# Splitting streamed weights into two parts: the low part by a negated copy and an adding transfer instead of a vector subtraction

## The chip, the cores and the metric

The kernel runs on one core of one Trainium2 chip. The metric is the device time of one execution in microseconds (us); lower is better. The kernel before took 1412.06 us (median of 3 runs, 1411.49 to 1412.78).

## The reference, cut to what matters

One inference step of a two-layer decoder trunk. 512 prompt tokens and 64 sample tokens (8 sequences of 8) go through it together as 576 columns. Each layer does

```
x = x + W_out . [SSD | sliding-window attention | HGRN2 | RG-LRU](W_in . RMSNorm(x))
x = x + W_down . square(relu(W_up . RMSNorm(x)))
```

with a model dimension of 1024, an input projection of 22 tiles of 128 columns (and four single columns), an output projection of 1024 x 1024 and a hidden layer of 4096. A final RMSNorm follows. All inputs are float32, and results are asked for in nearly full float32 precision. Caches and states of all four mixers are read and written too.

## The kernel before, in words

**The split.** A big product is done in the type float32r, which keeps fewer bits than float32. So that little is lost, each operand is written as hi + lo: hi is the operand rounded to float32r, lo is operand - hi. The product is then three matmuls, hi.hi, hi.lo and lo.hi, added up in PSUM. `product()` (L326 to L345) does this: for each half of the columns (288 of 576) it goes over the blocks of the contraction, and for each block it issues `wh.xh`, `wh.xl`, `wl.xh` in this order.

**The weights.** They stream from HBM in tiles of 128 x 1024 float32 (512 KB). `raw()` (L308) allocates a tile `raw` of a ring of WRAW = 3 buffers and loads it on the sync engine's queue. `weight()` (L315 to L324) allocates `hi` and `lo` of rings of WHL = 2 buffers and fills them with two instructions, both on line 323: ScalarE copies `raw` into `hi` (the store rounds), and VectorE subtracts `hi` from `raw` into `lo`. One such tile feeds 48 matmuls of 288 columns. "Plain" weights are those that go through `weight()`: 22 tiles of W_in, 8 of W_out, the first 6 of W_up and 32 of W_down per layer, without the last two of the second layer (these are split in `last_down()`): 134 in all. The other W_up tiles go through `up_pair()` (L1058), which forms a seven-product scheme with buffers of its own (`uh`, `ul`, `vh`, `vl`); it takes its raw tiles from the same ring.

**The order of the work.** A tile framework allocates the buffers, sets all semaphores, and orders each engine's instructions by a priority list; each engine then runs its own list in order. Both instructions of line 323 stand under `high_priority(HP)`, so they go ahead of other work that is ready at the time. Small loads and all stores but the last go through `dma()` (L167), on GpSimd's queue (POOL). A GpSimd instruction that waits holds up everything behind it on that engine.

**The stages.** Layer 0: mixers up to about 298 us (first projections and the norm, HGRN2 for one head pair, SSD, HGRN2 for the other pair, RG-LRU, attention, output projection), then its MLP up to about 709 us. Layer 1: mixers up to about 987 us, MLP and final norm to the end. In the mixers, the projections' products (`pi`) are mixed on TensorE with many small float32 matmuls of the mixers; in the MLP, groups of W_up products (`pu`, then `p`) alternate with groups of four W_down tiles (`pd`, 192 matmuls).

**The start.** The first weight (`w0`) is split before the norm: `norm()` (L356) is told to place its work behind the two instructions kept in `split_ins`; this is an order of issue, since in the trace the first norm activation starts before the first subtraction does. The first two products run ahead of 1/rms, which is worked out beside them.

Of the kernel before, what the change touches and what calls it, by code (L numbers as in the profile page):

```python
# [10 lines left out]
F32 = mybir.dt.float32  # L11
# [3 lines left out]
ALU = mybir.AluOpType  # L15
AX = mybir.AxisListType
PSUM = bass.MemoryType.PSUM
DRAM = bass.MemoryType.DRAM

DEPTH = 2  # L20
NP_ = 512                # prompt tokens
NB, NT = 8, 8            # sample sequences, tokens of each
NS = NB * NT
T = NP_ + NS             # token columns
# [5 lines left out]
NEG = -1e30  # L30
CW = 600                 # columns of a causal convolution over the padded row
PADW = CW + 3
SLOT = 608
WRAW, WHL = 3, 2
# [3 lines left out]
GROUPS = (288, 288)            # of columns at the end  # L38
AHEAD = 4
SQB = 2  # L40
ORDER = (0, 4, 1, 5, 2, 6, 3, 7)      # of the model dimension's tiles, as their products come
# [5 lines left out]
# columns of the packed per-layer vectors  # L47
# [9 lines left out]
# columns of the constants  # L57
# [7 lines left out]
# tiles of 128 columns of w_in, in the order of their use  # L65
# [48 lines left out]
class Pool:  # L114
    """A pool of tiles by role: t(tag) allocates the next tile of that role."""
# [15 lines left out]
def seqs(t, w=NT):  # L131
    """the sample columns as [rows, sequence, w]; w = 11 in padded rows"""
    o = NP_ if w == NT else NP_ + 3
    return t[:, o : o + NB * w].rearrange("p (b t) -> p b t", b=NB)


def staggered(parts):
    """run the parts' steps so that each part is one step behind the one before it"""
    n = 0
    while parts:  # L140
        n += 1
        for p in parts[:n]:
            if next(p, True):
                parts.remove(p)
                n -= 1


class Kern:
# [14 lines left out]
    # ---- small helpers  # L163
# [3 lines left out]
    def dma(self, dst, src):  # L167
        """a transfer that the first loads go before"""
        with self.tc.issue_after(self.gate):
            self.q(QS).dma_start(dst, src)  # L170
# [21 lines left out]
    # ---- constants and everything that is loaded once  # L192
# [36 lines left out]
    def spill(self):  # L229
        """the residual goes to DRAM while the mixers use its place"""  # L230
# [7 lines left out]
    def rel_bias(self):  # L238
        """bias[t, h, s] of a query t and the keys s of its own and the previous block, NEG outside the window."""
# [22 lines left out]
    def rel_bias_rows(self):  # L262
        nc, dma, (sel, newmask, skew) = self.nc, self.dma, self.rel
        for i in range(2):
# [3 lines left out]
            # sample rows (r, e, t) of 32-row groups: sequence b = 4 * u + r, head 2 * i + e  # L268
# [11 lines left out]
    def lower_bounds(self):  # L280
        """log of HGRN's lower bound of layer 1 and of its complement (layer 0's bound is zero by construction)."""
# [11 lines left out]
        V.tensor_tensor(t[1], t[1], t[3], op=ALU.mult)      # p0  # L293
        V.tensor_tensor(t[2], t[2], t[3], op=ALU.mult)      # p1
        V.tensor_tensor(t[3], t[1], t[2], op=ALU.add)
        V.tensor_tensor(t[3], t[3], t[1], op=ALU.subtract)
        V.tensor_scalar(t[3], t[3], 0.0, None, op0=ALU.max)  # lb
        V.tensor_scalar(t[4], t[3], -1.0, 1.0, op0=ALU.mult, op1=ALU.add)
        V.tensor_scalar(t[4], t[4], 0.0, None, op0=ALU.max)  # 1 - lb
# [7 lines left out]
    # ---- weights: float32 = hi + lo, both exact in float32r; eight blocks of 128 x 128  # L307
# [7 lines left out]
    def weight(self, src, raw=None):  # L315
# [6 lines left out]
        with self.tc.high_priority(HP):  # L322
            self.split_ins = nc.scalar.copy(hi, raw).ins, nc.vector.tensor_tensor(lo, raw, hi.bitcast(F32), op=ALU.subtract).ins  # L323
        return hi, lo  # L324

    def product(self, name, blocks, put):  # L326
        """put(half, columns, sum over the blocks (wh, wl, xh, xl) of w.T @ x in that half of the columns);
        behind a norm the first products run ahead of 1/rms, which their put() needs"""
# [21 lines left out]
    def exp_ln(self, ins):  # L350
        """the tables of exp and ln again, behind the last use of others"""
# [3 lines left out]
    # ---- RMSNorm over the model dimension: split (x * w) for the products, 1/rms as a factor of their results  # L355
# [31 lines left out]
    def rstd(self, r, sqs, scale, ones):  # L387
        """r = (mean over features + eps)^-1/2, on every partition; ones adds the rows that belong together."""
# [8 lines left out]
    # ---- input projection of one tile of columns -> [128, T] in PSUM, times 1/rms into dst  # L397
# [38 lines left out]
    def history(self, xp, hist, out):  # L436
        """the padded row's history columns, and the last three columns of each sequence as the new history"""
# [14 lines left out]
    def to_tokens(self, src, dst):  # L452
        """[128 features, T] -> tokens on partitions, [128, 4 x 128 | 128], the last block with 64 rows"""
# [10 lines left out]
    def by_sequence(self, dst, src):  # L464
        """dst [64, b, n] = src [64 tokens, n] in the rows of sequence b, else 0"""
# [4 lines left out]
    # ---- HGRN2, one pair of heads  # L470
    def hgrn_begin(self):
        P = self.hp = Pool(self, f"hgrn{self.li}", reuse_waits="tile")
        # zero-padded: entries outside a level's pattern stay zero
# [11 lines left out]
    def hgrn(self, p):  # L485
# [6 lines left out]
        # log sigmoid(f), log f, k  # L492
# [17 lines left out]
        # v with tokens on partitions  # L510
        vt = P.t("vt", 640)
        self.to_tokens(v, vt)
        # the diagonal: (q_t . k_t) v_t
# [8 lines left out]
        # pairs (s, t) by the level at which their blocks meet; every exponent is <= 0  # L522
# [37 lines left out]
        # c is now the running sum within a chunk  # L560
# [11 lines left out]
        # states  # L572
# [16 lines left out]
        # o  # L589
# [9 lines left out]
        # samples  # L599
# [16 lines left out]
        # the norm by head, the gate  # L616
# [8 lines left out]
    # ---- SSD  # L625
# [3 lines left out]
    def ssd_dt(self):  # L629
        """dt, the running sum of dt * A, and exp(last - sum): rows = heads"""  # L630
# [27 lines left out]
        # tokens on partitions: [128, chunk, (dt | sum | exp(last - sum)), head]  # L658
# [9 lines left out]
        # C's factor exp(sum) for the two heads of a group, and its last values  # L668
# [12 lines left out]
    def ssd(self):  # L681
# [29 lines left out]
        for g in range(2):  # L711
            rg = slice(64 * g, 64 * g + 64)
            # decay[s, t] = exp(sum_t - sum_s) where t >= s, times B_s . C_t
# [17 lines left out]
            # exp(min(., 0))  # L731
# [5 lines left out]
            # tokens on partitions: x dt, x dt exp(last - sum)  # L737
# [16 lines left out]
            # the states before each chunk and after the last one  # L754
# [19 lines left out]
            # y  # L774
# [32 lines left out]
    # ---- RG-LRU  # L807
    def lru(self, xps, gs):
# [4 lines left out]
        # -8 softplus(-lambda)  # L813
# [12 lines left out]
        for p, xp in enumerate(xps):  # L826
# [8 lines left out]
            V.tensor_scalar(r[:, p, :CW], r[:, p, :CW], lr[:, p : p + 1], None, op0=ALU.mult)      # log a  # L835
        # gelu's tanh
# [13 lines left out]
        # 1 - a^2 = tanh(-log a) (1 + a^2)  # L850
# [6 lines left out]
        # the column before a sample's first token carries its state  # L857
# [15 lines left out]
    # ---- sliding-window attention; q tile e holds heads (e, 2 + e) on the partitions of kv heads (0, 1)  # L873
    def swa(self, Q, K, Vv):
# [23 lines left out]
        # samples: rows (r, e, t) in groups of 32, blocks (i, u), sequence b = 4 * u + r  # L898
# [7 lines left out]
        Ls = [P.t("L", [2, 256], bufs=4) for _ in range(2)]      # by kv head  # L906
# [31 lines left out]
        p2 = self.bank("aos")                            # [128 (i d), u, r, 32]  # L938
# [9 lines left out]
        # prompt, by blocks of queries  # L948
# [3 lines left out]
        def block(nb):  # L952
# [3 lines left out]
            L = [P.t("L", [2, 256], bufs=4) for _ in range(2)]       # by kv head  # L956
# [44 lines left out]
    # ---- output projection of two mixers' tiles  # L1001
# [26 lines left out]
    # ---- MLP; its first product by the seven products of Winograd's form, quadrants of 2 feature halves x 2 column halves  # L1028
    def quads(self, P):
        """x * w in split quadrants: T1 = B12 - B11 in the place of B12, T2 = B22 - T1, T3 = B22 - B12, T4 = B21 - T2"""  # L1030
# [27 lines left out]
    def up_pair(self, P, i, Q, rstd):  # L1058
        """squared relu of two tiles of the hidden layer"""
# [9 lines left out]
        with self.tc.high_priority(HP):  # L1069
            a = split(hl("u", 8, 3), ra)                                       # A11 | A12  # L1070
            s = P.t("s", [8, 128])
            V.tensor_tensor(s[:, :4], rb[:, :4], rb[:, 4:], op=ALU.add)         # S1 = A21 + A22
# [308 lines left out]
```

## Time and profile before

| what | value |
|---|---|
| median of 3 runs | 1412.06 us |
| span of the profiled execution | 1412.2 us |
| TensorE (PE) matmuls | 1388.7 us, 98% |
| TensorE weight loads (PEld) | 1326.4 us, 94% |
| VectorE (DVE) | 1031.7 us, 73% |
| ScalarE (ACT) | 651.7 us, 46% |
| GpSimd (POOL) | 64.6 us, 5% |
| sync engine's DMA queue | 102.12 MB, 21.2% of the 16 DMA engines' span |
| GpSimd's DMA queue | 22.65 MB, 4.7% |

The profiled execution's span is 0.1 us above the median of the runs, so a sum made against the span stands for the median too. A busy share is an average over stages with different limits. Matmuls overlap in the pipeline: a busy time of 296 ns for one does not mean that the next one starts 296 ns later, so the count of matmuls in a stretch tells more than their busy time.

### The profile page before, as it was taken

The page shows a single profiled execution, that of the slowest core. Times are in us where ns is not written, and L with a number is a line of the kernel's source. Part 1 is how long each engine was busy: PE and PEld are TensorE (multiplying, and loading weights), DVE is VectorE, ACT ScalarE, POOL GpSimd, SP SyncE. Part 2 cuts the span into 40 slices and gives each one's busy share as a digit, 9 for nine tenths or more (in the row PEclk, how much of TensorE's full clock was granted, in tenths as well). Part 3 has the DMA queues.
Part 4 walks back from the last instruction along what each step waited for, and adds up shares of the span by engine and source line. Part 5 has one row for each costly group of instructions (what it writes and reads, how often), then busy time and mean ns, then how long its engine had stood idle before and what let it go on. Part 6 is the DMA issues. An engine that isn't in the chain of part 4 may idle for free.

```text
span 1412.2 us, 25457 instructions
## 1 busy us (share of the span) xinstructions
PE 1388.7 (98%) x10376; PEld 1326.4 (94%) x10376; DVE 1031.7 (73%) x2059; ACT 651.7 (46%) x1167; POOL 64.6 (5%) x125
## 2 busy tenths in 40 slices
PE   7999999999999999999999999999999999999997
PEld 7898889899999999999998989898999999999997
DVE  7966687668777778777668768764886877778765
ACT  6455427566433344333453734456662433343334
POOL 4010101100000000000000000010000000000000
PEclk9999999999999999999999999999999999999999
DMA  7142323312232223232330323130232223223221
GB/s 252 47 145 101 103 72 103 99 58 89 79 103 93 88 76 105 75 104 85 125 128 27 118 77 107 66 136 31 83 113 75 76 91 105 80 72 105 90 75 67
DMA packets 39716, 131.33 MB, mean 93 GB/s; under 512 B 5960, under 2 KB 8128, under 8 KB 39568
## 3 DMA queue, kind: packets, MB, share of 16 engines
q1 hardware_dynamic: 29312, 102.12, 21.2%
q0 software_dynamic: 6544, 22.65, 4.7%
q10 hardware_dynamic: 3744, 4.95, 1.0%
q8 instruction: 81, 1.33, 0.4%
q14 instruction: 35, 0.29, 0.1%
HBM read 120.32 MB, written 11.34 MB: 93 GB/s over the span
## 4 chain that ended last, share of the span: by engine, by line
PE 90%; DVE 4%; ACT 3%; issue 1%; DMA 1%; DVEq 0%; ACTq 0%
PE pd L336 33%; PE p L1089 21%; PE pi L336 16%; PE pu L336 5%; PE sc L544 2%; PE pl L1241 2%; PE ss L393 1%; PE ao L993 1%; PE y L781 1%; PE pdt L336 1%; PE o L595 1%; DMA cs<-acd 1%; PE os L605 1%; ACT hi L323 1%; PE ys L791 1%
## 5 line engine op out<-in xcount | busy, mean ns | idle before, releaser
L336 PE MATMUL pd<-fh,hi 128*128 128x288 f32 x960 | 283.8, 296 | 0.0
L336 PE MATMUL pd<-fl,hi 128*128 128x288 f32 x960 | 283.7, 296 | 0.0
L336 PE MATMUL pd<-fh,lo 128*128 128x288 f32 x960 | 283.6, 295 | 0.0
L323 ACT CAST hi<-raw 128x1024 fp32r<-128x1024 f32 x134 | 140.3, 1047 | 287.2 <-PE pd L336 154.6
L336 PE MATMUL pi<-xh,hi 128*128 128x288 f32 x704 | 213.4, 304 | 7.4 <-ACT xh L368 7.4
L336 PE MATMUL pi<-xl,hi 128*128 128x288 f32 x704 | 214.0, 304 | 0.7 <-DVE xl L369 0.7
L336 PE MATMUL pi<-xh,lo 128*128 128x288 f32 x704 | 213.9, 304 | 0.0
L323 DVE TENSOR_TENSOR lo<-raw,hi 128x1024 fp32r<-128x1024 f32 x134 | 163.6, 1221 | 24.3 <-ACT hi L323 23.4
L336 PEld LDWEIGHTS pd<-fh,hi 128*128 128x128 f32 x960 | 181.1, 189 | 0.0
L336 PEld LDWEIGHTS pd<-fl,hi 128*128 128x128 f32 x960 | 181.0, 189 | 0.0
L336 PEld LDWEIGHTS pd<-fh,lo 128*128 128x128 f32 x960 | 180.6, 188 | 0.0
L1024 DVE TENSOR_TENSOR x<-x,pd 128x288 f32<-128x288 f32 x240 | 107.9, 450 | 99.5 <-PE pd L336 99.3
L336 PEld LDWEIGHTS pi<-xh,hi 128*128 128x128 f32 x704 | 136.1, 194 | 11.7 <-ACT xh L368 7.4
L336 PEld LDWEIGHTS pi<-xh,lo 128*128 128x128 f32 x704 | 136.2, 193 | 4.2 <-issue 3.2
L336 PEld LDWEIGHTS pi<-xl,hi 128*128 128x128 f32 x704 | 135.9, 193 | 2.9 <-DVE xl L369 1.2
L1089 PE MATMUL p<-Th,ul 128*128 128x288 f32 x312 | 92.0, 295 | 0.0
L1089 PE MATMUL p<-Th,uh 128*128 128x288 f32 x312 | 92.0, 295 | 0.0
L1089 PE MATMUL p<-Tl,uh 128*128 128x288 f32 x312 | 92.0, 295 | 0.0
L1089 PE MATMUL p<-xh,ul 128*128 128x288 f32 x312 | 91.9, 295 | 0.0
L1089 PE MATMUL p<-xl,uh 128*128 128x288 f32 x312 | 91.7, 294 | 0.0
L1089 PE MATMUL p<-xh,uh 128*128 128x288 f32 x312 | 91.7, 294 | 0.0
L1065 ACT CAST uh<-raw 128x1024 fp32r<-128x1024 f32 x52 | 54.5, 1048 | 66.8 <-PE p L1089 44.1
(487 smaller groups left out, 3114.1 us busy)
## 6 DMA issues: line engine op xcount, KB each, us to landing
raw<-in_wu SPq DMA_DIRECT2D x64, 512.0 KB, 3.2
raw<-in_wd SPq DMA_DIRECT2D x64, 512.0 KB, 4.3
raw<-in_wi SPq DMA_DIRECT2D x44, 512.0 KB, 3.3
raw<-in_wo SPq DMA_DIRECT2D x16, 512.0 KB, 3.2
x<-in_xT SPq DMA_DIRECT2D x8, 288.0 KB, 5.5
a<-acd ACTq DMA_DIRECT2D x4, 576.0 KB, 3.9
xl<-in_xT POOLq DMA_DIRECT2D x8, 288.0 KB, 4.2
xd<-x POOLq DMA_DIRECT2D x8, 288.0 KB, 2.4
```

The costliest lines, as they stand in the source:

```text
L323: self.split_ins = nc.scalar.copy(hi, raw).ins, nc.vector.tensor_tensor(lo, raw, hi.bitcast(F32), op=ALU.subtract).ins
L336: self.nc.tensor.matmul(out, w, x[:, a], start=n == 0, stop=n == last)
L393: nc.tensor.matmul(ps[:, :TH], ones, s[:, TH * h : TH * h + TH], start=n == 0, stop=n == len(sqs) - 1)
L544: nc.tensor.matmul(pv[:, :, 64 * ci : 64 * ci + 64], kE[:, 128 * ci : 128 * ci + 128], qE[:, :, 64 * ci : 64 * ci + 64], start=True, stop= ...
L595: nc.tensor.matmul(ps[r, a], vt[:, 128 * ci + 64 * d : 128 * ci + 64 * d + 64], A[:, d, a], start=True, stop=ci == 0)
L605: nc.tensor.matmul(p2[r, NT * b : NT * b + NT], S0[r, b], q[r, NP_ + NT * b : NP_ + NT * b + NT], start=False, stop=b == NB - 1)
L781: nc.tensor.matmul(ps[r, a], xs[:, 128 * ci + 64 * j : 128 * ci + 64 * j + 64], D[j][:, a], start=True, stop=ci == 0)
L791: nc.tensor.matmul(p2[r, NT * b : NT * b + NT], S0T[rg, b, j], self.cs[j][rg, a], start=False, stop=b == NB - 1)
L1024: self.nc.vector.tensor_tensor(y[:, a], x[:, a], ps, op=ALU.add)
L1065: S.copy(hl[0], src)
L1089: nc.tensor.matmul(ps[:, :TH], u, x, start=j == 0, stop=j == 11)
L1241: nc.tensor.matmul(ps, u[:, o + q], v[:, a], start=j == 0, stop=j == 11)
```

## The change

The subtraction on VectorE goes. ScalarE writes `lo` as the rounded weights times -1, reading `raw` a second time. Then GpSimd issues a transfer from SBUF to SBUF that adds `raw` onto `lo`, so that `lo` = raw - hi. `split_ins` now holds ScalarE's copy and that transfer. The rings grow: 4 raw tiles and 3 pairs of hi and lo, which is 12 KB more of each SBUF partition; the space that the program reserves for GpSimd's DMA descriptors is set to 4096 bytes per partition. The rest of the diff removes comments.

```diff
-WRAW, WHL = 3, 2
+WRAW, WHL = 4, 3
...
         with self.tc.high_priority(HP):
-            self.split_ins = nc.scalar.copy(hi, raw).ins, nc.vector.tensor_tensor(lo, raw, hi.bitcast(F32), op=ALU.subtract).ins
+            first = nc.scalar.copy(hi, raw).ins
+
+            nc.scalar.mul(lo, raw, -1.0)
+            self.split_ins = first, nc.gpsimd.dma_start(lo, raw, accum_op=ALU.add).ins
         return hi, lo
...
-    nc = _bacc.Bacc("TRN2", target_bir_lowering=False, num_devices=1)
+    nc = _bacc.Bacc("TRN2", target_bir_lowering=False, num_devices=1, dynamic_dma_scratch_size=4096)
```

## Rows read from the trace of the kernel before

**Rows 1.** The page: span, and busy time of each engine.

```profile
span 1412.2 us, 25457 instructions
PE 1388.7 (98%) x10376; PEld 1326.4 (94%) x10376; DVE 1031.7 (73%) x2059; ACT 651.7 (46%) x1167; POOL 64.6 (5%) x125
```

**Rows 2.** Windows by stage: length, busy us (count) of five engines, clock, DMA share, GB/s.

```profile
0.00:298.00 298.00, 285.17 (x2100) 254.71 (x2100) 211.23 (x491) 154.13 (x301) 39.50 (x75) 0.97 0.33 113
298.00:709.00 411.00, 411.00 (x3092) 410.55 (x3092) 310.87 (x561) 172.98 (x285) 7.10 (x13) 1.00 0.27 92
709.00:987.00 278.00, 275.56 (x2065) 246.03 (x2064) 194.17 (x431) 143.72 (x275) 17.96 (x37) 0.97 0.25 84
987.00:1412.00 425.00, 416.96 (x3126) 415.15 (x3124) 315.47 (x578) 180.88 (x306) 0.00 (x0) 0.99 0.25 86
```

**Rows 3.** The chain that ended last, two pieces of layer 0's MLP: start, us, what.

```profile
371.80 25.49 PE pd L336 x192
397.29 22.30 PE p L1089 x168
```

**Rows 4.** Line 323: durations (ns, min/median/max), and one of ACT's waits (us, times).

```profile
L323 ACT CAST hi<-raw x134: 1027/1049/1083, 5.6 to 1375.8; 128x1024 fp32r<-128x1024 f32 x134
L323 DVE TENSOR_TENSOR lo<-raw,hi x134: 1205/1221/1227, 6.9 to 1377.5; 128x1024 fp32r<-128x1024 f32 x134
...
  PE pi L336: 35.8, 26
```

**Rows 5.** Timeline of the start: start, us, engine, line, operation, out<-in.

```profile
5.65 1.03 ACT L323 CAST hi<-raw 128x1024 fp32r<-128x1024 f32 x1
...
6.92 1.23 DVE L323 TENSOR_TENSOR lo<-raw,hi 128x1024 fp32r<-128x1024 f32 x1
...
9.33 0.44 PE L336 MATMUL pi<-xh,lo 128*128 128x288 f32 x1
...
13.89 0.37 PE L336 MATMUL pi<-xh,hi 128*128 128x288 f32 x1
...
14.21 1.03 ACT L323 CAST hi<-raw 128x1024 fp32r<-128x1024 f32 x1
...
17.49 1.05 ACT L323 CAST hi<-raw 128x1024 fp32r<-128x1024 f32 x1 [0.79 <-PE pi L336]
```

**Rows 6.** DMA issues: out<-in, queue, count, KB each, median us from issue to landing.

```profile
raw<-in_wi SPq DMA_DIRECT2D x44, 512.0 KB, 3.3
...
xl<-in_xT POOLq DMA_DIRECT2D x8, 288.0 KB, 4.2
...
kc<-in_kcT POOLq DMA_DIRECT2D x2, 512.0 KB, 4.9
vc<-in_cache_v POOLq DMA_DIRECT2D x2, 512.0 KB, 5.6
...
cst<-in_con POOLq DMA_DIRECT2D x1, 228.0 KB, 3.3
```

**Rows 7.** Windows behind the start, columns as in rows 2.

```profile
7.00:18.00 11.00, 9.92 (x53) 9.58 (x54) 10.78 (x14) 10.03 (x16) 5.86 (x9) 1.00 0.88 331
18.00:32.00 14.00, 13.52 (x98) 13.08 (x98) 10.30 (x20) 7.84 (x17) 7.08 (x12) 1.00 0.66 216
32.00:44.00 12.00, 11.91 (x89) 10.28 (x87) 11.11 (x24) 8.70 (x14) 0.00 (x0) 1.00 0.37 129
```

**Rows 8.** Pieces of line 323 on the chain in the mixers: start, us, what.

```profile
33.31 1.22 DVE lo L323
...
256.19 1.13 DVE lo L323
...
82.11 1.05 ACT hi L323
...
937.18 0.95 ACT hi L323
```

**Rows 9.** GpSimd's timeline: start, us, line, operation, idle time before and its releaser.

```profile
68.77 0.58 POOL L170 DMA_DIRECT2D out_phg<-hst  x1 [37.07 <-DVE hst L585]
...
83.34 0.54 POOL L170 DMA_DIRECT2D wdt<-in_wdt  x1
```

## The prediction, made before the changed kernel was run

> **What bounds the kernel now.** I read the page first: TensorE is busy 98% of a span of 1412.2 us, VectorE 73%, ScalarE 46% [rows 1]. That alone says that taking work off VectorE can pay only where TensorE waits, so the windows by stage come next. In the two MLP stages TensorE runs without a hole: 411.0 us of 411.00, and 416.96 of 425.00 with the final norm in it [rows 2]. The chain shows the pace there: 192 matmuls in 25.49 us and 168 in 22.30 us [rows 3], 132.8 ns each, so a weight tile with its 48 matmuls lasts 6.37 us. In the mixers, 298 and 278 us, TensorE is busy for 285.17 and 275.56 us, but at fewer matmuls per us (2100 in 298 us, where the pace would give 2244), part of it because small float32 matmuls take longer per instruction. What the change can win lies in these 576 us alone. The span stands 0.1 us from the median of the runs, so the sum against the span holds for the median too.
>
> **Part 1: the subtraction leaves VectorE.** 134 times 1.221 us [rows 4] is 163.6 us. 74 of them are tiles of W_up and W_down: 90 us that buy nothing, since TensorE has no hole in the MLP. The other 60, the tiles of W_in and W_out, are 73 us of VectorE time that matter only where the chain goes through them. On the chain in the mixers I find four whole pieces of it, 1.13 to 1.23 us each, of which the rows show the first and the last [rows 8]. The first two (2.45 us together) lie near 33 and 40 us; there TensorE is nearly full all the same, with 98 matmuls in 14 us and 89 in 12 us where the pace gives 105 and 90 [rows 7], so at most some 8 matmuls, 1.0 us, can be won. The other two (2.3 us), in the attention of layer 0, where VectorE hands its results to ScalarE and then to TensorE, I count in full. Gain 3.3 us; at least 0, at most the 4.7 us of the four pieces.
>
> **Part 2: ScalarE passes over each tile twice.** The second pass has the shape of the first, 1.05 us [rows 4], 134 times 141 us. In the MLP ScalarE is busy 172.98 of 411 and 180.88 of 425 us [rows 2], and the pass costs nothing as long as the low part is not late (part 4). In the mixers 60 passes, 63 us, come onto an engine that is half busy (154.13 of 298, 143.72 of 278). Beyond the start, ScalarE's copy is on the chain seven times, from 82.11 to 937.18 us, 0.94 to 1.05 us each [rows 8], 6.9 us in all. If every split stays where it is, each gets a second pass behind it: 7 times 1.05 us, 7.3 us slower. Against this, the third pair of buffers frees ScalarE from standing at the copy until TensorE gives a buffer back, 35.8 us in 26 waits [rows 4], so the splits can move into its idle time. I take the half, 3.6 us, with 0 and 7.3 us as the ends.
>
> **Part 3: the adding transfer itself.** The trace of before has no transfer from SBUF to SBUF and none that adds. The nearest rows are GpSimd's: 288 KB land 4.2 us after the issue, 512 KB after 4.9 and 5.6 us [rows 6]. The step from 288 to 512 KB is 0.7 us, 3.1 ns per KB, so 512 KB more cost 1.6 us. The adding transfer reads two tiles for the one it writes, so I take 4.9 + 1.6 = 6.5 us, an estimate. The lower end is 3.3 us, a plain tile on the sync queue, the upper end 11.2 us, twice the slowest row of 512 KB.
>
> **Part 4: the low part is later; is that covered?** Before, lo is there 1.05 + 1.22 = 2.3 us behind the raw tile. Now it takes 1.05 + 1.05 + 6.5 us, 8.6 us, and GpSimd's issue lies in the last term. With three pairs, the split of a tile may begin when the tile three places ahead has been used, two tile times (12.7 us) before it is needed. So in steady running the longer way is hidden, with 4.1 us to spare; the fourth raw buffer gives the transfer time to read its source. If the cover goes, three tiles share one round of 2.1 + L + 6.37 us (L is the landing), and TensorE waits once L is above 10.6 us. In the MLP I therefore count 0. The same transfers load GpSimd's queue with 134 issues of about 0.55 us, 74 us on an engine that is busy for 64.6 us [rows 1]; the loads and stores behind them are late by that at most, and none of those I find on the chain. The DMA engines are 25 to 33% busy by stage, at 84 to 113 GB/s [rows 2], so about 0.3 of their time for 100 GB/s; 134 tiles of 0.524 MB, read twice each, are 141 MB over the span, 100 GB/s, and some 0.3 more, which leaves room.
>
> **Part 5: the start, where nothing is in stock.** The first copy runs from 5.65 to 6.68 us, the first lo is ready at 8.15, and the first matmul that needs it starts at 9.33 us [rows 5]. Afterwards: copy to 6.68, second pass to 7.73, landing 6.5 us later, 14.2 us. In between TensorE has only the first hi matmuls. Before, the matmuls of this product started every 0.24 us up to 13.89 us [rows 5] and every 0.13 us from there on (the granted clock reads 1.00 in the whole stretch [rows 7]); of the 48 matmuls of this tile the last ended near 17.45 us, when the third copy got its buffer [rows 5]. I let TensorE start as slowly again: from 14.2 us on, the same 4.6 us (9.33 to 13.89) at the slow spacing give 19 matmuls, the other 25 take 3.3 us: 22.1 us, 4.7 us later. The second tile's copy starts at 14.21 us [rows 5]; its lo lands at 14.2 + 2.1 + 6.5 = 22.8, half a us after TensorE wants it. Sum 5.2 us. With a landing of 3.3 us it is 2.0, with 11.2 us it is 9.9 us. TensorE is full right behind this, so the hole stays.
>
> A rule speaks for more here. In the stretch from 7 to 18 us the DMA engines are 88% busy with the first loads [rows 7], yet a constant of 228 KB that GpSimd issued in it landed after 3.3 us [rows 6], not later than transfers of its size elsewhere. The Trainium skill (DMA: Bandwidth & Descriptors, section Queues, rings and completion order) says that each DMA engine goes round the queues that have work, a packet of each in turn; by that the addition would get half of each engine here, its 3.2 us of moving two tiles would become 6.4, and the sum below would be 3.2 us larger, 1420.9. I keep the row's answer.
>
> **Sum.** 1412.2 + 5.2 (start) - 3.3 (VectorE) + 3.6 (ScalarE) = 1417.7 us, 0.4% slower. Its own ends: 2.0 - 4.7 + 0 gives 1409.5, 9.9 - 0 + 7.3 gives 1429.4.
>
> **Rivals.** (a) Faster. The freed VectorE and the third buffer pair take all of line 323 off the chain in the mixers, on both engines, with a short landing: 2.0 - 4.7 - 6.9 = -9.6 us, 1402.6; with half of the 6.9 us, 1406. It decides where VectorE sets the end, in the attention and HGRN2 stretches, and wins from the point where more than the start's hole (2.0 to 5.2 us) comes back. For it speak VectorE's 11.11 us of 12 behind the start [rows 7]; against it, that TensorE is full in that very stretch. (b) No change: the hole of 5.2 us is made up by the 4.7 us of the chain's subtractions, and ScalarE's second pass falls into idle time: 1412.7. (c) The transfer is slow, L above 10.6 us. At 16 us a tile's round is 24.5 us for three, 8.2 us each instead of 6.37, and over the 28 tiles that follow one another without a break (6 of W_up and 8 of W_out in each layer) that is 51 us: 1463. (d) Order on GpSimd: an addition stands behind an instruction that waits for the mixers. The longest such waits in the mixers are 37 us [rows 9] and the like; two prepared tiles cover 12.7 of them, so a single one costs 24 us, 1436 with nothing else. Against it: the list is not in program order (the second layer's small load `wdt` goes out at 83.34 us, in the middle of layer 0 [rows 9]), and the addition has high priority.
>
> **How the numbers follow.** Forecast 0.42 (0.38 slower by over 0.2%, 0.04 less than that), (a) 0.30, (b) 0.18, (c) 0.07, (d) 0.03. About 0.2%, 2.8 us, is what a measurement of this kernel can tell from no change. Faster 0.30, the same 0.22, slower 0.48. The likeliest case alone spans 1409.5 to 1429.4; the range reaches down to (a)'s far end, 1402, and up to 1432, which leaves most of (c) and (d) out.
>
> **What would show it.** Right: the MLP stages keep 25.49 us per 192 matmuls; VectorE loses 164 us and ScalarE gains 141; the first `wl.xh` matmul starts near 14 us and the 48th ends near 22 us; the additions land after 5 to 8 us. Wrong: matmuls with `lo` waiting for a DMA in the middle of the MLP (then c), additions issued long after their second pass has ended (then d), or fewer us in the mixers in spite of the late start (then a). The prediction falls if the first product is no later than before, or if the mixers give back more than 5 us.

## The result and the profile after

The changed kernel takes 1469.32 us (median of 4 runs, 1462.35 to 1472.59); the kernel before, on the same chip, 1412.42 us (4 runs). The ratio is 1.0392, 95% interval 1.0364 to 1.0419: some 57 us slower, far above the range predicted. The profiled execution took 1462.35 us, with a span of 1460.4 us, 48.2 us more than that of [rows 1]; the readings below account for these 48.2 us. The three other executions took 6 to 10 us more, and no trace of them was kept.

The page of the kernel after: span, busy time by engine, two DMA queues; then three costly groups (instructions | busy, mean ns | idle before, and what ended it); and two lines of the list of its DMA issues (count, KB, median us to landing).

```profile
span 1460.4 us, 25815 instructions
...
PE 1409.8 (97%) x10376; PEld 1339.8 (92%) x10376; DVE 880.3 (60%) x1925; ACT 790.1 (54%) x1310; POOL 178.5 (12%) x259
...
q0 software_dynamic: 25840, 92.91, 30.0%
q1 hardware_dynamic: 29312, 102.12, 20.4%
...
L326 POOL DMA_DIRECT2D lo<-raw x134 | 116.1, 866 | 1112.4 <-ACT lo L325 860.4
...
L339 PE MATMUL pi<-xh,lo 128*128 128x288 f32 x704 | 213.2, 305 | 7.4 <-DMA lo<-raw 7.4
...
L325 ACT ACTIVATE lo<-raw 128x1024 fp32r<-128x1024 f32 x134 | 141.1, 1053 | 0.0
...
lo<-raw POOLq DMA_DIRECT2D x134, 512.0 KB, 4.8
...
cst<-in_con POOLq DMA_DIRECT2D x1, 228.0 KB, 6.3
```

The work moved as the change says: VectorE is busy 151 us less than in [rows 1], ScalarE 138 us more, GpSimd 114 us more. TensorE's 10376 matmuls, the same number, were busy for 21 us more than before, and its idle time grew from 23.5 to 50.6 us. The surprising line is the second of the three groups, the matmuls that read a low weight part: TensorE was ready and waited for an addition's landing for 7.4 us in the whole program, in one wait. Landing is quick, 4.8 us in the median. So some 40 of the 48 us were lost without TensorE itself standing at the new transfer.

The first of the windows by stage, columns as in [rows 2]:

```profile
0.00:298.00 298.00, 269.75 (x1885) 237.96 (x1885) 171.69 (x423) 159.62 (x270) 59.84 (x101) 0.91 0.57 156
```

In the first 298 us TensorE did 1885 matmuls where it had done 2100. The same times hold different work from there on, so I cut by landmarks of the timeline instead (the start of the first `pu` matmul of each layer, and of layer 1's first `pi`). In the kernel before, the output projection runs on to 321.1 us, so that [rows 2] counts its last 23 us to the MLP; here they belong to the mixers. Later tables use this cut; all of it is from profiled executions.

| us | mixers 0 | MLP 0 | mixers 1 | MLP 1 and end | span |
|---|---|---|---|---|---|
| before | 321.1 | 388.3 | 303.8 | 399.0 | 1412.2 |
| after | 353.2 | 395.0 | 310.4 | 401.8 | 1460.4 |
| difference | 32.1 | 6.7 | 6.6 | 2.8 | 48.2 |

**The MLP's pace held.** The chain of after has the same pieces as [rows 3]:

```profile
410.40 25.75 PE pd L339 x192
436.15 22.30 PE p L1092 x168
```

What the MLPs lost they lost before this, in their first groups.

**The start.** The chain of after through the first split (start, us, what) answers to [rows 5]; the line under it is the window of the first 20 us:

```profile
6.61 0.97 ACT lo L325
...
7.88 9.47 DMA lo<-raw
...
17.40 13.41 PE pi L339 x80
```

```profile
0.00:20.00 20.00, 4.30 (x15) 3.61 (x16) 10.86 (x41) 16.50 (x30) 8.44 (x18) 1.00 0.93 306
```

The first addition took 9.47 us, twice the median, and the first low matmul starts at 17.40 instead of 9.33 us. The 48th matmul of the projections starts at 25.76 us (17.29 before). The DMA engines were busy for 93% of the first 20 us.

**The SSD stretch.** The chain of before, and then of after, where SSD's small matmuls come (`su`, `sus`, `y`, `ys`):

```profile
119.12 1.05 PE sus L770 x2
120.18 8.02 PE pi L336 x59
128.20 0.58 PE y L781 x4
```

```profile
125.15 1.63 PE sus L773 x2
...
127.35 1.08 PE y L784 x4
...
145.18 1.94 PE su L761 x8
147.12 3.22 PE pi L339 x15
```

Before, 59 projection matmuls stand between `sus` and `y` and TensorE is full. After, there are none: a product's six high matmuls run at 119.5 to 120.2 us, and its first low matmul stands behind this whole section of SSD (that of the first head group), at 147.05 us, though the addition for it (issued at 109.06 us) had landed at 117.07 us. It is the list of TensorE that has it there. With the stretch so thin the granted clock falls, as windows of before and after show (columns as in rows 2):

```profile
120.00:140.00 20.00, 20.00 (x148) 17.28 (x148) 13.57 (x26) 7.70 (x11) 0.98 (x3) 0.92 0.27 96
140.00:160.00 20.00, 20.00 (x126) 15.77 (x126) 11.86 (x26) 5.32 (x9) 1.08 (x2) 0.84 0.14 44
```

```profile
120.00:140.00 20.00, 16.13 (x80) 9.95 (x79) 8.55 (x21) 6.15 (x9) 2.34 (x5) 0.64 0.57 175
140.00:160.00 20.00, 18.54 (x108) 14.15 (x108) 9.93 (x23) 3.09 (x5) 0.00 (x0) 0.76 0.06 23
```

A granted clock of 0.64 is a mean over the two levels, 2.4 and 1.2 GHz; four `y` matmuls that take 0.58 us before take 1.08 us here.

**GpSimd's queue.** Its timeline in after (start, us, what, and the idle time before with what ended it) answers to [rows 9]:

```profile
93.68 0.86 POOL L326 DMA_DIRECT2D lo<-raw  x1 [18.74 <-ACT lo L325]
94.22 0.90 POOL L170 DMA_DIRECT2D out_phg<-hst  x1
...
107.99 0.56 POOL L170 DMA_DIRECT2D wdt<-in_wdt  x1
```

`out_phg` went out at 68.77 us before and goes out at 94.22 us now, right behind an addition that stood waiting 18.74 us for ScalarE, though VectorE had made its data by 74.95 us. `wdt` moved from 83.34 to 107.99 us. Twice the chain itself goes from an addition over the small transfers behind it, where the chain of before goes through none of these:

```profile
100.60 0.44 POOL lo L326
...
101.17 2.29 DMA skew<-x
...
107.12 0.74 POOL x L170
...
107.99 2.78 DMA wdt<-in_wdt
```

```profile
181.39 1.06 ACT lo L325
...
182.74 0.85 POOL lo L326
183.59 0.58 POOL S L170
184.17 0.46 POOL out_pssm L170
...
184.92 6.17 DMA x<-skew
```

The first piece leads on to SSD's data; TensorE, full until then, stands 1.18 and 2.12 us at its end (before `xts` and `su`). At the end of the second it stands 3.2 us.

### The profile page after: what moved, and what is told of

Its sections match the earlier page's. It is cut to its first block, busy times and chain, and to the rows that moved or that the text cites. A ratio compares the mean times of both kernels' runs of the same rounds, so it can differ in the third digit from the quotient of the medians.

```text
span 1460.4 us, 25815 instructions
## 1 busy us (share of the span) xinstructions
PE 1409.8 (97%) x10376; PEld 1339.8 (92%) x10376; DVE 880.3 (60%) x1925; ACT 790.1 (54%) x1310; POOL 178.5 (12%) x259
## 3 DMA queue, kind: packets, MB, share of 16 engines
q0 software_dynamic: 25840, 92.91, 30.0%
q1 hardware_dynamic: 29312, 102.12, 20.4%
## 4 chain that ended last, share of the span: by engine, by line
PE 83%; ACT 5%; DVE 4%; issue 3%; DMA 3%; POOL 0%; DVEq 0%; ACTq 0%; POOLq 0%
PE pd L339 31%; PE p L1092 19%; PE pi L339 15%; PE pu L339 2%; PE pl L1244 2%; PE sc L547 2%; PE ss L396 1%; ACT lo L325 1%; DMA lo<-raw 1%; PE ao L996 1%; PE y L784 1%; ACT hi L323 1%; PE ys L794 1%; PE pdt L339 1%; PE y L786 1%
## 5 line engine op out<-in xcount | busy, mean ns | idle before, releaser
L326 POOL DMA_DIRECT2D lo<-raw x134 | 116.1, 866 | 1112.4 <-ACT lo L325 860.4
L325 ACT ACTIVATE lo<-raw 128x1024 fp32r<-128x1024 f32 x134 | 141.1, 1053 | 0.0
```

The source lines that it names most:

```text
L325: nc.scalar.mul(lo, raw, -1.0)
L326: self.split_ins = first, nc.gpsimd.dma_start(lo, raw, accum_op=ALU.add).ins
```

## The experiments

Theories. **H1**: TensorE's planned order puts low matmuls behind the mixers' small ones. **H2**: the start. **H3**: additions that wait hold up small transfers on GpSimd's queue. **H4**: the raw ring stands still until an addition has landed. Rivals: the new rings, ScalarE's second pass, the additions' traffic. All diffs are against the changed kernel, cut to what matters; a change of indentation alone is not marked. Ratios are to the kernel before, with 95% intervals. Every edit is planned anew, so the lists of all engines can change with it.

### Where the loss lies

**New rings, old subtraction.**

```diff
-            nc.scalar.mul(lo, raw, -1.0)
-            self.split_ins = first, nc.gpsimd.dma_start(lo, raw, accum_op=ALU.add).ins
+            self.split_ins = first, nc.vector.tensor_tensor(lo, raw, hi.bitcast(F32), op=ALU.subtract).ins
```

> The subtraction on VectorE as before, with the new rings (4 raw, 3 hi and lo) and the new descriptor reserve. Theory H1 (TensorE's planned order: with the addition, the list puts the low matmuls of a W_in tile behind the mixers' small matmuls), H2 (the first additions land late) and H3 (additions hold up small loads on GpSimd's queue) all make this kernel equal to before: 1409 to 1414 us. Rival R1 (the rings or the reserve cost the time by themselves): 1440 to 1470 us.

Measured 1426.78 us, 1.0075 (1.0049 to 1.0100). Neither: the rings by themselves cost about 11 us (7 to 14), without any transfer.

**Transfer in the MLP alone; transfer in the mixers alone.** The flag is set for the length of the MLP (for the second kernel the condition is reversed).

```diff
+            if self.mlp_now:
                 nc.scalar.mul(lo, raw, -1.0)
                 self.split_ins = first, nc.gpsimd.dma_start(lo, raw, accum_op=ALU.add).ins
+            else:
+                self.split_ins = first, nc.vector.tensor_tensor(lo, raw, hi.bitcast(F32), op=ALU.subtract).ins
```

> The negated pass and the adding transfer for the MLP's weights alone (74 of 134 tiles: 6 of W_up and 31 of W_down per layer on average); the mixers' W_in and W_out tiles are subtracted on VectorE as before; new rings. H1, H2 and H3 put all of the loss into the mixers: 1409 to 1416 us. R2 (the additions' traffic or ScalarE's second pass slows any stage in proportion to its tiles): 74/134 of the 57 us, so about 1443 us.

> The adding transfer for W_in and W_out alone (60 of 134 tiles), subtraction on VectorE in the MLP. H1, H2 and H3: nearly all of the loss stays, 1460 to 1472 us; as to the 6 us that the first MLP products lost beyond the mixers' loss, if those come from additions of W_up tiles the result is nearer 1460. R2 (in proportion to the tiles): about 1437 us.

Measured 1431.26 us, 1.0103 (1.0073 to 1.0133), and 1461.54 us, 1.0319 (1.0283 to 1.0355). The first lies above its range, which did not yet know the rings' 11 us; the second lies in it. Against the kernel with the new rings, the MLP's additions cost 4.5 us, which the runs alone do not tell from nothing, and the mixers' 35. The rival in proportion to the tiles (74 of 134 would be 23 of the 42.5 us that the transfer costs beyond the rings) falls. The MLP's own part is not nothing, though:

| us | mixers 0 | MLP 0 | mixers 1 | MLP 1 and end |
|---|---|---|---|---|
| new rings, subtraction | 334.7 | 388.7 | 304.9 | 399.3 |
| transfer in the MLP alone | 329.4 | 394.9 | 304.4 | 401.2 |
| transfer in the mixers alone | 357.3 | 389.6 | 313.2 | 399.3 |

In no profiled execution without the transfer in the MLP does the first MLP take more than 389.6 us, and in none with it less than 390.9.

**ScalarE's second pass, without a transfer.**

```diff
-            self.split_ins = first, nc.gpsimd.dma_start(lo, raw, accum_op=ALU.add).ins
+            self.split_ins = first, nc.vector.tensor_tensor(lo, raw, lo.bitcast(F32), op=ALU.add).ins
```

> ScalarE writes the negated rounded weights as in the change, and VectorE adds the raw ones onto them: no transfer, rings and reserve as in the change. H1, H2, H3 (the transfer is the cause): the time of the kernel with the new rings and the subtraction, 1426.8 us, plus 0 to 7 us for the second pass: 1427 to 1434 us. R4 (ScalarE's second pass is the cause): 1450 to 1470 us.

Measured 1424.30 us, 1.0078 (1.0047 to 1.0108), as with the rings and the subtraction: of the second pass nothing is seen. The two intervals leave room for some 6 us either way, so a cost of a few us is not excluded.

### The start and the order

**First four weights subtracted.**

```diff
+            self.nw += 1
+            if self.nw > 4:
                 nc.scalar.mul(lo, raw, -1.0)
                 self.split_ins = first, nc.gpsimd.dma_start(lo, raw, accum_op=ALU.add).ins
+            else:
+                self.split_ins = first, nc.vector.tensor_tensor(lo, raw, hi.bitcast(F32), op=ALU.subtract).ins
```

> The changed kernel, but the first four weights of the program are subtracted on VectorE, the rest goes by the transfer. H2 (lateness at the start, 8.2 us at the end of the first product pair in the trace, carried to the end): 1458 to 1463 us, and TensorE's first low matmul near 9.4 us instead of 17.4. If a later wait would have absorbed the lateness: 1466 to 1472 us.

Measured 1454.96 us, 1.0306 (1.0257 to 1.0355): by the ratios 12 us less than the changed kernel, with some 8 us either way, so it is not told apart from what H2 said. In the profiled executions it is 9.1 us: the first low matmul starts at 9.35 us, the mixers of layer 0 take 341.4 instead of 353.2 us, those of layer 1 3.0 us more. The start's lateness is carried to the end; whether more hangs on it is not shown here.

**Low matmuls last in each half**, with the transfer, and as a control with the subtraction.

```diff
-            for wh, wl, xh, xl in blocks:
...
+            pairs = [(w, x) for wh, wl, xh, xl in blocks for w, x in ((wh, xh), (wh, xl))]
+            for w, x in pairs + [(wl, xh) for wh, wl, xh, xl in blocks]:
```

> The changed kernel, but each half of a product issues its 16 matmuls with the high weights first and its 8 with the low ones behind them, so that the low part is due 16 matmuls (about 2.1 us) after the product begins. The list of TensorE then has 103 other instructions between the last high and the first low matmul of the input projections' halves, where the changed kernel has 651 and the kernel before 76. H1: most of the 28 us that the projections' stretch of layer 0 lost and part of layer 1's 9 come back, the start's 8 stay: 1425 to 1440 us. R3 (landings that TensorE waits for): the trace of after shows 7.4 us of such waits, so 1461 us at the best. H3 (small loads behind waiting additions): no change, 1460 to 1470 us.

> The subtraction on VectorE with the new rings, and low matmuls last in each half: the control for the run with the transfer and low matmuls last (1438.6 us). Of the other instructions between the high and the low matmuls of the projections' halves the list has 5 (new rings and subtraction in the old order: 41). H1 (putting them last helps only because the transfer makes the low part late): as the kernel with the new rings, 1422 to 1430 us. Rival (this order is faster by itself, whatever makes the low part): 1400 to 1412 us.

Measured with the transfer 1438.60 us, 1.0168 (1.0133 to 1.0204), and with the subtraction 1421.11 us, 1.0039 (1.0024 to 1.0055). The first came out as H1 said: 31 us come back, and `out_phg` still goes out at 94.57 us, as late as in after, so H3's held stores are not what cost these 31 us. But the control is 5.7 us faster than the kernel with the new rings, just outside what either theory gave: about a fifth of the gain is this order's own, or that of the list that comes with it.

**Both: first four subtracted, and low matmuls last.**

> Low matmuls last in each half and the first four weights subtracted on VectorE. If H1 and H2 add up: 1438.6 us less what the start still loses there (at most 5 us, as 46 instead of 68 matmuls ran in the first 20 us, 22 x 0.13 = 2.9 us, and some of 140 follow), so 1433 to 1437 us. TensorE's list has 209 instructions in the gaps instead of 103, which by H1 costs some of it: up to 1442 us.

Measured 1443.91 us, 1.0206 (1.0189 to 1.0223), 2 us above the upper end. The 48th matmul starts at 17.74 us (20.27 with the low ones last alone), yet the whole is 5 us slower. In the profiles the mixers of layer 0 gain 0.9 us and those of layer 1 lose 2.2; the two MLPs lose 8.5. So gaps in the projections' list are not the reason there, and the reason was not found. Mends do not add up where each one makes a new plan.

**Small transfers off GpSimd's queue**; then that with the first four weights subtracted; then with the low matmuls last as well.

```diff
-QS, QC = 'gpsimd', 'scalar'
+QS, QC = 'sync', 'scalar'
```

> The changed kernel with the small loads and stores issued by the sync engine, so that GpSimd's queue holds the additions and some fills only. The planned list of TensorE then has 115 other instructions between the high and the low matmuls of the input projections' halves (changed kernel 651, before 76): the late low matmuls were planned because additions and small transfers share GpSimd's queue. H1 (the list) and H3 (GpSimd's queue), which this run cannot tell apart, both give 1430 to 1445 us, with the start's 8 us staying. If the time is in the additions themselves (their landing, their traffic, ScalarE's pass): 1460 to 1470 us. A third outcome is that the small transfers now wait behind weight loads on the sync engine's queue, which waits for raw buffers: above 1470 us.

> The transfer and the new rings with two of the three mends: the first four weights subtracted on VectorE, and the small loads on the sync engine's queue; the matmuls of a half in their old order. TensorE's list has 53 instructions in the gaps of the projections' halves, fewer than the kernel before (76). H1 and H2 (a list with few gaps and an early start are all that is needed): as with all three mends, 1424 to 1434 us. If the low matmuls must also come last, because they wait for landings although the list is good: the run with the small loads moved alone, 1453.4 us, less the 8 to 14 us of the start: 1439 to 1446 us.

> The transfer and the new rings with three mends at once: the first four weights subtracted on VectorE, low matmuls last in each half, small loads on the sync engine's queue (8 instructions in the gaps of the projections' halves). If start, order and GpSimd's queue are all that the transfer costs in the mixers, what is left is the new rings' loss (1426.8 us) and the MLPs' starts (6.8 + 2.8 us in the trace of after): 1431 to 1437 us. If the mixers lose to something else too (the additions' traffic): 1440 to 1455 us.

Measured 1453.37 us, 1.0271 (1.0251 to 1.0291); 1440.31 us, 1.0170 (1.0142 to 1.0198; its profiled run was the fastest of five, 1432.83 us); and 1427.58 us, 1.0086 (1.0058 to 1.0114).

| us | mixers 0 | MLP 0 | mixers 1 | MLP 1 and end |
|---|---|---|---|---|
| small transfers on sync | 339.6 | 393.6 | 315.0 | 405.7 |
| and first four subtracted | 319.5 | 392.5 | 317.2 | 401.6 |
| and low matmuls last | 324.9 | 390.9 | 305.5 | 408.4 |

The first lies between its ranges, 8 us above the one and 7 below the other. The second lies in the range of its rival (1439 to 1446), the third 3 us below the lower of its two. The second's profile, 6 to 9 us faster than the four other executions of that kernel, says where the time goes: with the start mended and GpSimd's queue left to the additions, the mixers of layer 0 take 319.5 us, where they took 321.1 before. Its chain has the projections back between `sus` and `y`:

```profile
116.65 1.05 PE sus L776 x2
117.70 7.76 PE pi L342 x57
125.46 0.58 PE y L787 x4
```

So in this execution nothing is left of the 32 us of that stage, the rings' part included. The additions from the fifth on are all there, with their traffic and their landing, and cost nothing in it; TensorE waits for no landing anywhere, so the rival's reason (low matmuls that wait for landings) is not seen. Where the other executions lose their 6 to 9 us, no trace shows.

In layer 1 the same kernel loses 13.4 us. The projections stand between `sus` and `y` there too (64 matmuls), but then TensorE stands. Its timeline, and the window behind it:

```profile
833.29 0.69 DVE L777 TENSOR_TENSOR S<-S,acj 128x512 f32<-128x512 f32 x1 [4.21 <-DMA S<-in_sS]
833.90 1.41 DVE L741 TENSOR_TENSOR a<-a,b 128x1024 f32<-128x1024 f32 x2
...
835.23 1.09 PE L787 MATMUL y<-a,c 128*64 128x128 f32 x4 [4.11 <-issue]
```

```profile
835.00:851.00 16.00, 15.78 (x78) 11.22 (x79) 3.64 (x8) 0.68 (x1) 0.00 (x0) 0.50 0.12 42
```

VectorE's list has an update of SSD's state (`S`), which waits for one of the moved small loads, ahead of the product `a` that `y` reads. TensorE stands 4.11 us for it, and then runs SSD's small matmuls at a granted clock of 0.50, the lower of the two levels throughout: 16.2 us from the first `y` to the end of the next `xt`, where before it was 10.8. Together that is 9.5 of the 13.4 us. The kernel with only the small transfers moved has the same wait (4.0 us before `y`). With all three mends VectorE's list has `a` ahead of `S`, TensorE does not stand there, and the mixers of layer 1 take 305.5 us. As a whole that kernel stands where the new rings with the subtraction stand; the 9.4 us of its last stage are the next section's.

### The rings

**The reserve alone; the fourth raw tile alone** (both with the subtraction).

```diff
-WRAW, WHL = 4, 3
+WRAW, WHL = 3, 2
```

```diff
-WRAW, WHL = 4, 3
+WRAW, WHL = 4, 2
```

> The subtraction on VectorE and the old rings (3 raw, 2 hi and lo), with the new descriptor reserve of 4096 bytes alone; every engine's list is that of the kernel before, instruction by instruction. R1a (the lists that the larger rings give cost the 10 to 13 us of the kernel with the new rings): 1410 to 1416 us. R1b (the smaller reserve slows GpSimd's transfers): 1420 to 1430 us, with GpSimd's issues longer than the 0.52 to 0.58 us of before.

> The subtraction on VectorE, 4 raw tiles, but 2 pairs of hi and lo as before. TensorE's list differs from before in 6 lines, ScalarE's in 240, VectorE's in 668 (with the third pair: 171, 462, 1052). If the third pair of hi and lo makes the loss, since splits then run earlier, ahead of the mixers' own work on ScalarE: 1410 to 1416 us. If the fourth raw tile makes it (earlier weight loads beside the small loads): 1420 to 1430 us.

Measured 1414.32 us, 0.9996 (0.9983 to 1.0009), and 1415.27 us, 1.0000 (0.9985 to 1.0014). Neither costs anything that these runs can tell (some 2 us); what costs the 11 us, in the plan that comes with it, is the third pair of hi and lo. A sign of how: SSD's decay rows go through DRAM (`acd`, `cs`) on ScalarE's queue. In the timeline and the chain of before the store goes out, and the last load runs, so:

```profile
69.89 0.52 ACTq L657 DMA_DIRECT2D acd<-c  x1
...
87.93 5.55 DMA cs<-acd
```

and with the new rings so:

```profile
79.10 0.51 ACTq L658 DMA_DIRECT2D acd<-c  x1
...
92.10 10.30 DMA cs<-acd
```

In ScalarE's list the store now stands behind three activations that it stood ahead of. That this is the cause was not isolated.

**The transfer with the old rings** (the first diff of this section) **and the old reserve.**

> The negated pass and the transfer with the old rings and reserve. If the rings cost their 10 to 13 us in the changed kernel too and earn nothing there: about 1456 us. If the rings are needed because an addition holds a raw tile until it has landed (4.5 us longer than the subtraction does): the MLP's first groups and the mixers lose more, 1475 to 1500 us. TensorE's list has 739 instructions in the gaps (changed kernel 651).

Measured 1535.44 us, 1.0835 (1.0803 to 1.0868), beyond both. ScalarE's waits in it (us in total, times, longest) say what is short:

```profile
ACT hi L323 <- DMA raw<-in_wd: 156.1, 26, 8.3
ACT hi L323 <- PE pd L338: 96.0, 38, 5.7
```

**The MLP's transfer with other rings**: 6 raw tiles and 2 pairs, then 3 raw tiles and 3 pairs.

> The transfer for the MLP's weights alone, with 6 raw tiles and 2 pairs of hi and lo (as many bytes as 4 and 3). Theory H4: with the transfer, the start of each MLP loses about 6 and 2 us because the raw ring stands still until additions land (a raw load issued at 372.44 us right behind a landing at 372.39, TensorE's chain through it). H4 gives back these: the first MLP's stretch, from the first W_up product to layer 1's first product, 388 to 390 us instead of 394.9, the second's 391 instead of 392.9. Rival: the additions' traffic delays the weight loads whatever the ring: 394 to 396 us again. The mixers' stretch depends on the list and is not part of this test.

> The transfer for the MLP's weights alone, 3 raw tiles and 3 pairs of hi and lo: TensorE's list is that of the same kernel with 4 raw tiles, instruction by instruction. H4 (raw tiles held until additions land make weight loads late): the first MLP's stretch grows from 394.9 us to 400 us or more, and the second's too. Rival H5 (the pairs of hi and lo are what is short, the raw ring is not): 394 to 397 us again.

Measured 1451.11 us, 1.0250 (1.0226 to 1.0273), and 1507.17 us, 1.0632 (1.0602 to 1.0662).

| us, MLP's transfer alone | MLP 0 | MLP 1 and end |
|---|---|---|
| 4 raw, 3 pairs | 394.9 | 401.2 |
| 6 raw, 2 pairs | 402.8 | 414.3 |
| 3 raw, 3 pairs | 428.4 | 438.4 |

The first lies above both its ranges and does not test H4: TensorE waits there for landings, 15.8 us in 17 waits before `pu` and `pd`, and never with 4 raw tiles and 3 pairs, so with the transfer two pairs are short by themselves. The second speaks for H4: the same list of TensorE, one raw tile less, and 33.5 us more in the first MLP. Its chain is the ring's round:

```profile
391.10 4.47 DMA lo<-raw
...
395.62 3.19 DMA raw<-in_wd
...
401.19 4.55 DMA lo<-raw
```

An addition lands, the load into its raw tile goes out at once, copy and pass follow, and the next addition goes out: 10.09 us for a tile that TensorE uses up in 6.37. The round goes one tile at a time because a pair of W_up tiles holds the two other raw tiles; in the timeline the pair's two loads go out, and the first of the two tiles is read for the last time, so:

```profile
386.76 1.29 SPq L312 DMA_DIRECT2D raw<-in_wu  x2
...
421.73 0.69 DVE L1071 TENSOR_TENSOR vl<-raw,vh 128x512 fp32r<-128x512 f32 x1 [3.37 <-ACT vh L1070]
```

With four raw tiles two are left to share the round, 5.0 us per tile (an estimate: half of 10.09). With the subtraction one would do: a load of 3.2, a copy of 1.05 and a subtraction of 1.22 us [rows 4] are 5.5 us (an estimate). With four raw tiles the chain goes through weight loads and additions only near an MLP's beginning (in before it goes through neither anywhere). Two pieces of it, one of the kernel with the MLP's transfer alone, one of that with all three mends:

```profile
372.44 6.09 DMA raw<-in_wu
```

```profile
1063.38 5.83 DMA raw<-in_wu
```

Each is a load of W_up that goes out as an addition gives its raw tile back. The MLPs in which they lie lose 6 and 9 us by the tables; that the whole of it comes from such loads was not shown.

**The kernel before, low matmuls last** (old rings and reserve, subtraction).

> The kernel before with low matmuls last in each half (subtraction, 3 raw, 2 pairs, old reserve): does any of this make a kernel faster than before? H1: 1408 to 1418 us, since the low part was not late there. If the order is faster by itself: under 1405 us.

Measured 1420.71 us, 1.0030 (1.0017 to 1.0042), a little above the range. No kernel tried is faster than before.

## Why the prediction was wrong

The side was right (slower, 0.48), the size was not: 1417.7 us forecast, 1432 the upper end, 1469.3 measured. The side owes little to the mechanism: of the 48 us, some 8 came the way that was forecast.

**Parts 1 and 2** were right in what they moved (VectorE -151, ScalarE +138; 164 and 141 were said). ScalarE's second pass, counted at 3.6 us, was not seen (1424.3 against 1426.8 us without it, some 6 us either way). VectorE's gain of 3.3 us showed nowhere. The count of ScalarE's copies on the chain left out one, at 38.56 us; nothing hangs on it.

**Part 3** estimated 6.5 us for the landing; the median was 4.8 us. It took one number for the whole program, and at the start it was 9.47.

**Part 5, the start**, was mis-sized: 4.7 us said at the 48th matmul (5.2 in all), 8.5 measured. The term that failed is the first landing, 9.47 us for 6.5, at a DMA share of 93%, with no transfer ahead of it on GpSimd's queue. I had kept the row of `cst`, a 228 KB load that took 3.3 us in that stretch; behind the addition the same load now took 6.3. The Trainium skill's rule (DMA: Bandwidth & Descriptors, section Queues, rings and completion order: engines go round the queues, packet by packet) would have given 6.5 + 3.2 = 9.7 us, an estimate. The trace agrees that the landing is longer beside the first loads; that the number fits so well is partly luck, since the 6.5 in it was 1.7 us above the median landing. That the hole stays, as the prediction said, held in the sense that the start's lateness was not made up later. What hangs on it differs with the plan: by the ratios, mending the start gave back 12 us from the changed kernel and 14 with the small transfers moved, and lost 5 with the low matmuls last (each with some 5 to 8 us either way).

**Part 4, "is that covered?"**, is the step that failed most. It set the landing against the time of the tiles in stock, as if the engines took their work as it becomes ready. Landing was covered, as reckoned: TensorE's one wait for it, 7.4 us, is at the start. But each engine runs a list, and the list had changed; as I read it, because in the plan the low part is late and GpSimd's queue is shared (what the plan assumes for a landing was not read out). In that list the low matmuls went behind SSD's, and the mixers lost their filling and with it the clock: 32.1 and 6.6 us in the mixers, of which some 8 are the start's and some 15 also show with the new rings alone. I had looked for the opposite order on GpSimd, an addition behind a waiting small transfer (rival d). What came was small transfers behind a waiting addition, which my sentence "none of those I find on the chain" had dismissed: 2.78 us of `wdt` and 6.17 us of `x<-skew` on the chain, at whose ends TensorE stood for some 6.5 us. The issues themselves took 0.87 us each, 116 us, where 0.55 and 74 were said; GpSimd stayed 12% busy. "In the MLP I count 0" held in the steady part; at each MLP's beginning it left out that the same four raw tiles also serve the W_up tiles of the other scheme, and that a raw tile is loaded again only a landing plus 3.2 us after its second pass: 6.7 and 2.8 us.

**The rings** I had only as a help (buffers for ScalarE, cover for the transfer). The third pair costs about 11 us in the plan that comes with it, though the transfer needs it: without the larger rings it is some 65 us slower still.

**Rivals.** (a) and (b) needed a start of 5 us at most and gains in the mixers; neither was there. (c) fell: landing is 4.8 us in the median and 9.9 at the most, below 10.6. (d) had the right queue and the wrong order.

**Open.** Why the third pair's plan is slower, and where most executions of the kernel with two mends lose 6 to 9 us against its profiled one. H1 and H3 were never tried each by itself: moving the small transfers changes list and queue together. The run with low matmuls last separates them only in part, as its control moved too.

## What to carry to other kernels

Asking whether a longer latency is covered by the stock of prepared tiles is not enough where a planner writes each engine's list: look also at where the late consumer, and everything that shares the new instruction's queue, will stand in the list, and at what filled the holes there before. The list of an engine that is not the bottleneck counts too: one instruction of VectorE that waits for a load, put ahead of one that TensorE needs, cost 4.1 us and the clock behind it. A transfer that reads a ring's tile holds it until it has landed; count its round (load, passes, landing) against the pace of the consumer, with all users of the ring. And a buffer more is a new plan, not a free good: time the rings alone, with the old operations, before crediting or blaming the rest.

## What the runs showed of the hardware

The adding transfer of 512 KB from SBUF to SBUF lands after 4.5 us at the least, 4.8 in the median, 9.9 at the most, about as soon as plain loads of that size on GpSimd's queue in before (medians of two loads each, 4.9 and 5.6 us [rows 6], single ones 3.7 to 6.1). It is dear in the DMA engines' time: GpSimd's queue went from 22.65 MB and 4.7% to 92.91 MB and 30.0%. The 70.26 MB of the additions thus took about 25% of the engines' span, where 102.12 MB of weights took 20.4%, 1.8 times as much per byte written. Each occupies GpSimd for 0.87 us at the issue, where small transfers take some 0.55 us in before.

In one stretch TensorE did 64 projection matmuls in 8.69 us, stood 4.11 us, and then had only SSD's small matmuls: the granted clock there was 0.50, and they took 16.2 us. The same matmuls behind 60 projection matmuls without the wait, in before, took 10.8 us.
